# The first MLP product as seven half-size products per pair of columns, and the MLP in two passes through memory

## The chip, the cores and the metric

One NeuronCore of a Trainium2 chip runs the whole layer. The metric is the device time of one execution in microseconds. TensorE (PE) does the matrix products, with its weight loads shown as a lane of their own (PEld); VectorE (DVE) and ScalarE (ACT) do the elementwise work; GpSimd (POOL) has little to do; SyncE (SP) issues the transfers. All arithmetic is in float32: each operand of a product is split into a high part, rounded to the multiplier's format, and the remainder (low part), and every product is made of three matmuls, high times high, high times low and low times high.

## The reference, cut to what matters

The change is in the MLP at the end of the layer; what stands before it (attention, gating, the merge and `w_out`) keeps its arithmetic.

```
# x: (512, 2048) tokens by channels, g_ff: (2048), w_ff1: (2048, 8192), w_ff2: (8192, 2048)
h2 = x * rsqrt(mean(x * x) + EPS) * g_ff          # RMSNorm, one scale per token
x  = x + square(relu(h2 @ w_ff1)) @ w_ff2
```

## The kernel before

The program is written as a flow of tiles; a planner puts the instructions on the engines' queues by a simulated time, in the order of the program where several are ready, and gives out the buffers. Activations lie in slots of 128 partitions by 512 elements (`slot`, 72 in one pool and 10 in another). A weight tile of 512 KB (128 partitions by 1024 elements, `w_raw`) is loaded by SP, ACT rounds it to `w_hi`, DVE subtracts to get `w_lo`; there are six such pieces, so three weight tiles are ready or in use at a time. `mm3` issues the three matmuls of a product (lines 68, 69, 70).

Ahead of the MLP, `w_out` makes the new residual in 16 tiles `x2[tb, j]` (128 tokens by 512 channels, line 562), whose squares are summed (line 564). Each tile is turned (line 577) and split with the gain `g_ff` into `h2T` (lines 106 and 107), channels on the partitions and the 512 tokens along the row. The token scale `rstd_b` (the reciprocal root, lines 584, 585, 213, then 291 to 294) isn't in `h2T`: it is multiplied in later, when a hidden tile leaves PSUM.

The MLP is one loop over 16 chunks of 512 hidden columns. `hidden(f, p)` makes a pair of hidden tiles (2 times 128 columns by 512 tokens) by `by_column`: 16 channel tiles times 2 column tiles times 3 matmuls, each 512 tokens wide, 96 matmuls a pair. A hidden tile is clamped, scaled (line 603) and squared (line 604). `factors` (lines 615 to 618, and the splits 103, 104) makes seven factors of 256 tokens from a pair: the four quarters' three own ones and four sums, as in Winograd's form of Strassen's product. `strassen` multiplies these with seven factors of a block of `w_ff2` (512 hidden rows by 1024 channels): four loads of 512 KB, four sums on DVE (line 165), seven splits (lines 103, 104), and for each factor 12 matmuls 512 channels wide; each factor's result is added from PSUM into the residual tiles (line 643), 16 additions of 128 by 512 a call. So the product with `w_ff1` is direct, the product with `w_ff2` already takes seven parts in eight, and the two alternate: while the factors of one chunk are multiplied, the hidden tiles of the next are made.

The order of the work around the change is this: PE takes its matmuls in the order of the program; DVE and ACT prepare up to three weight tiles ahead; SP's queue is in order, and each load waits for a free `w_raw`.

Of the kernel before, what the change touches and what calls it, by code (L numbers as in the profile page):

```python
# [28 lines left out]
SLOTS = 72  # L29
SPARE = 10  # L30
# [3 lines left out]
def tile_hybrid_layer(ctx: ExitStack, tc: tile.TileContext, x, g_mix, w_in, g_q, g_k, ln_g, ln_b,  # L34
# [10 lines left out]
    before = ExitStack()  # L45
    spare = before.enter_context(tc.tile_pool(name="spare", bufs=SPARE))
# [25 lines left out]
    state = {"load": None}  # L72
# [10 lines left out]
    def weight(wap, kt, c0, w=W):  # L83

        ck = CK * W // w
        raw = wpool.tile([P, ck, w], F32, name="w_raw", tag="w_raw", bufs=3)
# [53 lines left out]
    def strassen(wap, r0, c0, lhs, evac):  # L140

        KH = 2

        def piece(name):
            return wpool.tile([P, KH, W], F32R, name=name, tag="w_piece", bufs=6)

        def whole(name):
            return state["whole"].tile([P, KH, W], F32, name=name, tag="whole")

        def quarter(h, c):
            raw = whole("w_raw")
            state["load"] = nc.sync.dma_start(
                out=raw, in_=wap[r0:r0 + 2 * KH * P, c0 + c * W:c0 + (c + 1) * W]
                .rearrange("(k h p) c -> h p k c", p=P, h=2)[h])
            return raw

        w11, w12, w21, w22 = quarter(0, 0), quarter(1, 0), quarter(0, 1), quarter(1, 1)
        sc = whole("w_sum")

        def plus(o, a, b):
            nc.vector.tensor_tensor(out=o, in0=a, in1=b, op=ALU.add)


        made = {"m7": lambda: plus(w11, w11, w21), "m6": lambda: plus(sc, w11, w22),
                "y22": lambda: plus(w12, sc, w12), "m5": lambda: plus(w21, w21, w22)}
        take = {"y11": w11, "y21": w12, "m7": w11, "m6": sc, "y22": w12, "m4": w22, "m5": w21}  # L170
        banks = {}
        for name, b, first, last in (("y11", 0, True, False), ("y21", 1, True, True),
                                     ("m7", 2, True, False), ("m6", 0, False, False),
                                     ("y22", 1, True, True), ("m4", 2, False, True),
                                     ("m5", 0, False, True)):
            if name in made:
                made[name]()
            hi, lo = piece("w_hi"), piece("w_lo")
            split_to(hi, lo, take[name])
            if first:  # L180
                banks[b] = [(aux if b == 1 else acc)("q") for _ in range(2)]
            for t in range(2):
                o = banks[b][t]
                for k in range(KH):
                    y = [part[:, t * P:(t + 1) * P] for part in lhs(k, name)]
                    mm3(o, y, (hi[:, k, :], lo[:, k, :]), first and k == 0, k == KH - 1,
                        skip_group_check=True)
                evac(name, t, o)
# [82 lines left out]
    def hT_of(k):  # L271

        if k == len(hT):
            t = aux("xT")
            for tb in range(NTB):
                nc.tensor.transpose(out=t[:, tb * P:(tb + 1) * P], in_=xq[tb, k], identity=ident)
            hT.append(split(t, "hT", gT[:, k:k + 1], spare if k < SPARE // 2 else slots))
        return hT[k]
# [264 lines left out]
    for j in range(D // W):  # L543
# [3 lines left out]
        def evac_b(c, o):  # L547
# [3 lines left out]
            mT.append(split(m, "mT", pool=spare if len(mT) >= KT - 4 else slots))  # L551
# [5 lines left out]
    h2T = []  # L557
    ss2 = const.tile([P, NTB, 4], F32, name="ss2")
    for j in range(D // W):
        def evac_x(tb, o):  # L560
            t = x2[tb, j]
            nc.vector.tensor_tensor(out=t, in0=o, in1=t, op=ALU.add)
            sq = slot("sq")
            nc.scalar.activation(out=sq, in_=t, func=AF.Square, accum_out=ss2[:, tb, j:j + 1])

# [8 lines left out]
        def turned(c, j=j):  # L574
# [5 lines left out]
            h2T.append(split(t, "h2T", gT2[:, k:k + 1]))  # L580
# [6 lines left out]
    behind.append(lambda: along(rstd2, rstd_b))  # L587

    before.close()
    state["whole"] = ctx.enter_context(tc.tile_pool(name="whole", bufs=5))  # L590


    HS = S // 2
    PAIRS = 2
    chunks = DFF // (PAIRS * 2 * P)

    def hidden(f, p):

        act = []

        def evac_f(c, o):
            t = slot("relu")
            nc.vector.scalar_tensor_tensor(out=t, in0=o, scalar=0.0, in1=rstd_b, op0=ALU.max, op1=ALU.mult)
            nc.scalar.activation(out=t, in_=t, func=AF.Square)
            act.append(t)

        by_column(w_ff1[0], (f * PAIRS + p) * 2 * P, lambda k: h2T[k], KT, evac_f, "f1", w=2 * P)
        return act

    def factors(act):  # L610
# [3 lines left out]
        m7, m6, m4, m5 = ta[:, :HS], ta[:, HS:], tb[:, :HS], tb[:, HS:]  # L614
        nc.vector.tensor_tensor(out=m7, in0=y12, in1=y22, op=ALU.subtract)
        nc.vector.tensor_tensor(out=m6, in0=m7, in1=y11, op=ALU.subtract)
        nc.vector.tensor_tensor(out=m4, in0=y21, in1=m6, op=ALU.add)
        nc.vector.tensor_tensor(out=m5, in0=y11, in1=y12, op=ALU.subtract)
        y = {}
        for name, src in (("y11", y11), ("y21", y21), ("m7", m7), ("m6", m6), ("y22", y22),  # L620
# [54 lines left out]
```

## Time and profile before

| | |
|---|---|
| median of 3 runs | 2540.3 us (2539.97 to 2541.31) |
| the profiled execution | 2540.31 us |
| its span, first to last instruction | 2538.6 us |
| PE busy | 2520.2 us (99%), 11306 matmuls |
| weight loads (PEld) busy | 2086.5 us (82%) |
| DVE busy | 1550.1 us (61%) |
| ACT busy | 851.6 us (34%) |
| POOL busy | 118.6 us (5%) |
| data moved | 259.83 MB, mean 102 GB/s |

The profile is one execution, taken by the hardware profiler. Its own time is 2540.31 us beside a span of 2538.6 us, so 1.7 us lie outside the span. An engine's busy time is the time in which at least one of its instructions ran. The duration of a matmul is modelled and longer than the time from one matmul's start to the next, since they are pipelined; the distance of starts is what counts for time. The same holds in a smaller measure for DVE and ACT, whose instructions overlap a little.

### The profile page before, as it was taken

The numbers are of one execution on the slowest core, as the hardware profiler recorded it, in microseconds if no ns is written. First come the engines' busy times: TensorE is split into PE (matmuls) and PEld (weight loads), VectorE is DVE, ScalarE is ACT, GpSimd is POOL, SyncE is SP. The second block draws the span as 40 slices with busy tenths as digits, with TensorE's granted clock in tenths as the row PEclk, the third lists the DMA queues.
The fourth block names the chain that finished last, engine by engine and source line by source line (L and its number), as shares of the span: only waits on it lengthen the run. The fifth ranks groups of instructions, "written<-read, shape, count | busy, mean of one in ns | idle before, by whom it ended". The sixth has DMA issues, their size and how long they took to land.

```text
span 2538.6 us, 28443 instructions
## 1 busy us (share of the span) xinstructions
PE 2520.2 (99%) x11306; PEld 2086.5 (82%) x11306; DVE 1550.1 (61%) x2062; ACT 851.6 (34%) x1172; POOL 118.6 (5%) x123
## 2 busy tenths in 40 slices
PE   8999999999999999999999999999999999999998
PEld 7888888888888888888888888888888888888886
DVE  4555463332335343333477877787877877787879
ACT  5333332222223222232333334243333334243332
POOL 0212110000121010100000000000000000000000
PEclk9999999999999999999999999999999999999999
DMA  5322323333333333333433333332333333332323
GB/s 175 92 86 73 91 67 100 92 100 100 109 99 100 94 98 99 116 125 108 125 91 117 99 101 100 100 117 85 114 99 117 99 101 100 100 116 86 114 74 117
DMA packets 169574, 259.83 MB, mean 102 GB/s; under 512 B 8368, under 2 KB 77024, under 8 KB 169440
## 3 DMA queue, kind: packets, MB, share of 16 engines
q1 hardware_dynamic: 169440, 258.01, 33.3%
q8 instruction: 89, 1.46, 0.2%
q14 instruction: 45, 0.37, 0.0%
HBM read 253.78 MB, written 4.19 MB: 102 GB/s over the span
## 4 chain that ended last, share of the span: by engine, by line
PE 96%; DVE 2%; issue 1%; DMA 0%; ACT 0%; POOL 0%; SPq 0%; DVEq 0%; POOLq 0%
PE f L70 9%; PE f L68 9%; PE f L69 9%; PE q L69 9%; PE q L68 9%; PE q L70 9%; PE xo L70 2%; PE xo L69 2%; PE xo L68 2%; PE gb L68 2%; PE gb L70 2%; PE gb L69 2%; PE ga L68 2%; PE ga L69 2%; PE ga L70 2%; PE v L70 1%
## 5 line engine op out<-in xcount | busy, mean ns | idle before, releaser
L92 DVE TENSOR_TENSOR w_lo<-w_raw,w_hi 128x1024 fp32r<-128x1024 f32 x336 | 413.6, 1234 | 672.6 <-ACT w_hi L90 663.8
L90 ACT CAST w_hi<-w_raw 128x1024 fp32r<-128x1024 f32 x336 | 353.9, 1053 | 944.4 <-PE q L69 149.1
L68 PE MATMUL f<-h2T_hi,w_hi 128*128 128x512 f32 x1024 | 398.5, 389 | 0.0
L69 PE MATMUL f<-h2T_lo,w_hi 128*128 128x512 f32 x1024 | 398.3, 389 | 0.0
L70 PE MATMUL f<-h2T_hi,w_lo 128*128 128x512 f32 x1024 | 393.9, 389 | 0.0
L69 PE MATMUL q<-w_lo,ys 128*128 128x512 f32 x896 | 349.9, 391 | 1.6 <-DVE w_lo L104 1.5
L70 PE MATMUL q<-w_hi,ys 128*128 128x512 f32 x896 | 349.3, 390 | 0.0
L103 ACT CAST w_hi<-w_raw 128x1024 fp32r<-128x1024 f32 x192 | 202.0, 1053 | 421.7 <-PE f L69 273.5
L643 DVE TENSOR_TENSOR x<-x,q 128x512 f32<-128x512 f32 x512 | 336.8, 683 | 3.5 <-PE q L70 0.6
L68 PE MATMUL q<-w_hi,ys 128*128 128x512 f32 x896 | 325.5, 390 | 4.2 <-ACT w_hi L103 4.2
L104 DVE TENSOR_TENSOR w_lo<-w_raw,w_hi 128x1024 fp32r<-128x1024 f32 x192 | 234.9, 1224 | 133.5 <-ACT w_hi L103 133.5
L70 PEld LDWEIGHTS f<-h2T_hi,w_lo 128*128 128x128 f32 x1024 | 192.3, 188 | 39.9
L69 PEld LDWEIGHTS f<-h2T_lo,w_hi 128*128 128x128 f32 x1024 | 192.3, 188 | 39.8
L68 PEld LDWEIGHTS f<-h2T_hi,w_hi 128*128 128x128 f32 x1024 | 192.2, 188 | 39.7
L68 PEld LDWEIGHTS q<-w_hi,ys 128*128 128x128 f32 x896 | 168.6, 188 | 40.2 <-ACT w_hi L103 5.4
L69 PEld LDWEIGHTS q<-w_lo,ys 128*128 128x128 f32 x896 | 168.7, 188 | 38.8 <-DVE w_lo L104 3.9
L70 PEld LDWEIGHTS q<-w_hi,ys 128*128 128x128 f32 x896 | 168.7, 188 | 34.8
L68 PE MATMUL gb<-hT_hi,w_hi 128*128 128x512 f32 x256 | 100.3, 392 | 0.2 <-DVE gb L413 0.2
L68 PE MATMUL xo<-w_hi,mT_hi 128*128 128x512 f32 x256 | 100.5, 393 | 0.0
L68 PE MATMUL ga<-hT_hi,w_hi 128*128 128x512 f32 x256 | 100.4, 392 | 0.0
L69 PE MATMUL ga<-hT_lo,w_hi 128*128 128x512 f32 x256 | 100.0, 391 | 0.0
L70 PE MATMUL ga<-hT_hi,w_lo 128*128 128x512 f32 x256 | 99.9, 392 | 0.0
(199 smaller groups left out, 3690.0 us busy)
## 6 DMA issues: line engine op xcount, KB each, us to landing
w_raw<-in_w_ff_dram SPq DMA_DIRECT2D x256, 512.0 KB, 3.7
w_raw<-in_w_in_dram SPq DMA_DIRECT2D x144, 512.0 KB, 3.7
w_raw<-in_w_out_dram SPq DMA_DIRECT2D x32, 512.0 KB, 3.7
w_raw<-in_w_oa_dram SPq DMA_DIRECT2D x16, 512.0 KB, 3.7
w_raw<-in_w_ob_dram SPq DMA_DIRECT2D x16, 512.0 KB, 3.7
x<-in_x_dram SPq DMA_DIRECT2D x16, 256.0 KB, 5.4
out_dram<-x SPq DMA_DIRECT2D x16, 256.0 KB, 2.0
xq<-in_x_dram SPq DMA_DIRECT2D x12, 256.0 KB, 6.5
```

The lines of the kernel that those rows point to most:

```text
L68: nc.tensor.matmul(o, lhsT=lh[0], rhs=rh[0], start=start, stop=False, **kw)
L69: nc.tensor.matmul(o, lhsT=lh[0], rhs=rh[1], start=False, stop=False, **kw)
L70: nc.tensor.matmul(o, lhsT=lh[1], rhs=rh[0], start=False, stop=stop, **kw)
L90: nc.scalar.copy(out=hi, in_=raw)
L92: nc.vector.tensor_tensor(out=lo, in0=raw, in1=f32(hi), op=ALU.subtract)
L103: nc.scalar.copy(out=hi, in_=src)
L104: nc.vector.tensor_tensor(out=lo, in0=src, in1=f32(hi), op=ALU.subtract)
L643: nc.vector.tensor_tensor(out=a, in0=a, in1=o, op=op)
```

## The change

Both MLP products are made of seven half-size products, and the MLP is two passes: first all of `w_ff1`, then all of `w_ff2`.

**First pass.** The normalized activations need the token scale before they are used, so `x2T` (turned, with the gain) is multiplied by `rstd_b` and cut into seven factors `hs` for each pair of channel tiles (128 rows by 256 tokens each). The first pair of hidden tiles is made directly, by matmuls 256 tokens wide, from the factors that need no sums; then the four sums are made for all eight pairs of channel tiles. Each of the other 31 pairs goes through `strassen_columns`: the weights of a block of 2048 rows by 256 columns come as four tiles of 512 KB (rows of 128 elements), the factors of the weights are made by three additions on DVE and one addition done by a transfer (`accum_op`, issued by POOL, onto the tile `w21`), seven splits, and 7 times 24 matmuls 256 tokens wide. Their results leave PSUM by four ACT copies and four DVE additions of 128 by 256; the hidden pair is clamped, squared, cut into its seven factors, and these are written to memory (`keep_hidden`, 7 writes of 256 KB a pair). The residual tiles are written to memory too (`kept`).

**Second pass.** `strassen_tokens` takes chunks of 1024 hidden rows by 1024 channels: two weight blocks whose results add up in PSUM, so each result is added into the residual once for 1024 hidden rows. The hidden factors of the next chunk are read back between the products (`fetch`), and the residual tiles are read back at the start of the pass.

The core of the diff:

```diff
-SLOTS = 72
-SPARE = 10
+SLOTS = 64
+LONG = 12
+SHORT = 6
...
+    BANK = {"y11": (0, True), "y21": (1, True), "m7": (2, True), "m6": (0, False), "y22": (3, True),
+            "m4": (2, False), "m5": (0, False)}
...
+        def parts(self, name):
+            if name == "m7":
+                nc.vector.tensor_tensor(out=self.a, in0=self.w11, in1=self.w21, op=ALU.add)
+
+                nc.gpsimd.dma_start(out=self.w21, in_=self.blocks[1, 1], accum_op=ALU.add)
+            if name == "m6":
+                nc.vector.tensor_tensor(out=self.c, in0=self.a, in1=self.w22, op=ALU.add)
+            if name == "y22":
+                nc.vector.tensor_tensor(out=self.w12, in0=self.c, in1=self.w12, op=ALU.add)
+            src = self.take[name]
+            hi, lo = piece("w_hi"), piece("w_lo")
...
+    def strassen_columns(wap, c0, rhs, evac):
+
+        KH = KT // 2
+        blocks = {(h, c): wap[:, c0 + c * P:c0 + (c + 1) * P].rearrange("(k h p) c -> h p k c", p=P, h=2)[h]
+                  for h in range(2) for c in range(2)}
+        w = Sums(blocks, [state["raw"].tile([P, KH, P], F32, name="w_raw", tag="w_raw") for _ in range(6)])
...
+            o = banks[b][:, :HS]
+            for k in range(KH):
+                mm3(o, (hi[:, k, :], lo[:, k, :]), rhs[name][k], new and k == 0, k == KH - 1,
+                    skip_group_check=True)
+            evac(name, o)
...
+            for i in range(2):
+                hi, lo = ws[i].parts(name)
+                for t in range(2):
+                    for k in range(KQ):
+                        y = [part[:, t * P:(t + 1) * P] for part in lhs[name][i * KQ + k]]
+                        mm3(banks[b][t], y, (hi[:, k, :], lo[:, k, :]), new and i == 0 and k == 0,
+                            i == 1 and k == KQ - 1, skip_group_check=True)
...
-            h2T.append(split(t, "h2T", gT2[:, k:k + 1]))
+            keep = slot("x2T")
+            nc.scalar.activation(out=keep, in_=t, func=AF.Copy, scale=gT2[:, k:k + 1])
+            x2T.append(keep)
...
-    behind.append(lambda: along(rstd2, rstd_b))
+    flush()
+    along(rstd2, rstd_b)
...
+    for b in range(KT):
+        y = x2T[b]
+        nc.vector.tensor_tensor(out=y, in0=y, in1=rstd_b, op=ALU.mult)
+        for half in range(2):
+            name = "y" + "12"[b % 2] + "12"[half]
+            far = name == "y11" or name == "y21" and b // 2 < LONG - KT // 2
+            hs[name, b // 2] = halves(y[:, half * HS:(half + 1) * HS], long if far else slots)
...
+        for i, name in enumerate(NAMES):
+            nc.sync.dma_start(out=store[p // GROUP][i, p % GROUP], in_=f32(ys[name, 0]))
...
+    for k in range(KT // 2):
+        factors(hs, x2T[2 * k:2 * k + 2], k)
+    keep_hidden(0, act)
...
+    for p in range(1, DFF // (2 * P)):
+        hidden(p)
...
+    first.close()
+    second = [ctx.enter_context(tc.tile_pool(name=n, bufs=6)) for n in ("raw2", "more2")]
+    state["raw"], state["more"] = second
+    lhs = {name: fetch(0, name) for name in NAMES}
+    for tb in range(NTB):
+        for j in range(D // W):
+            t = slot("x2")
+            nc.sync.dma_start(out=t, in_=kept[tb, j])
+            x2[tb, j] = t
```

## Rows read from the trace of the kernel before

**Rows 1.** The page's head and its busy time by engine.
```profile
span 2538.6 us, 28443 instructions
...
PE 2520.2 (99%) x11306; PEld 2086.5 (82%) x11306; DVE 1550.1 (61%) x2062; ACT 851.6 (34%) x1172; POOL 118.6 (5%) x123
```

**Rows 2.** Stretches of the span: engines' busy time, clock, DMA share, GB/s.
```profile
6.00:12.00 6.00, 3.51 (x13) 2.82 (x14) 3.28 (x4) 2.45 (x4) 0.00 (x0) 1.00 1.04 344
...
1297.00:1338.00 41.00, 41.00 (x182) 33.96 (x182) 30.80 (x44) 15.01 (x21) 0.00 (x0) 1.00 0.29 89
...
2466.00:2500.00 34.00, 28.78 (x118) 22.33 (x117) 33.37 (x55) 14.19 (x24) 0.00 (x0) 0.93 0.24 71
```

**Rows 3.** Groups by line in the MLP: matmuls of either product (one line of three).
```profile
L68 PE MATMUL f<-h2T_hi,w_hi 128*128 128x512 f32 x1024 | 398.5, 389 | 0.0
...
L68 PE MATMUL q<-w_hi,ys 128*128 128x512 f32 x896 | 325.5, 390 | 4.2 <-ACT w_hi L103 4.2
```

**Rows 4.** Timeline of PE where the MLP begins: start, duration, instruction.
```profile
1215.18 0.39 PE L68 MATMUL f<-h2T_hi,w_hi 128*128 128x512 f32 x1
...
1215.86 0.39 PE L68 MATMUL f<-h2T_hi,w_hi 128*128 128x512 f32 x1
```

**Rows 5.** Timeline of PE in attention, around three matmuls 256 wide.
```profile
160.60 0.29 PE L68 MATMUL z<-kT_hi,qT_hi 128*128 128x256 f32 x1
...
160.97 0.22 PE L68 MATMUL z<-kT_hi,qT_hi 128*128 128x128 f32 x1
```

**Rows 6.** Timeline of the weight loads in the position mixing.
```profile
782.61 0.19 PEld L527 LDWEIGHTS mix<-wsp,vn_hi 128*128 128x128 f32 x1
...
783.07 0.19 PEld L527 LDWEIGHTS mix<-wsp,vn_hi 128*128 128x128 f32 x1
```

**Rows 7.** Timeline and tile rows of the token scale, last residual tile to `rstd_b`.
```profile
1215.38 0.69 DVE L562 TENSOR_TENSOR x<-xo,x 128x512 f32<-128x512 f32 x1 [0.67 <-PE xo L70]
...
1218.03 1.02 POOL L213 TENSOR_TENSOR rstd<-ms,mhalf 128x4 f32<-128x4 f32 x1 [178.62 <-DVE ms L585]
...
L291 DVE TENSOR_SCALAR dg<-ident,rstd x4: 276/278/280, 1230.5 to 1231.1; 128x128 f32<-128x128 f32 x4
...
1236.25 0.69 DVE L294 COPY rstd_b<-rp 128x512 f32<-128x512 f32 x1 [0.61 <-PE rp L293]
```

**Rows 8.** Timeline of DVE late in the MLP.
```profile
2462.05 1.23 DVE L104 TENSOR_TENSOR w_lo<-w_raw,w_hi 128x1024 fp32r<-128x1024 f32 x1 [0.56 <-ACT w_hi L103]
...
2473.65 0.42 DVE L615 TENSOR_TENSOR m<-relu 128x256 f32<-128x256 f32 x1
2473.99 0.42 DVE L618 TENSOR_TENSOR m<-relu 128x256 f32<-128x256 f32 x1
...
2480.06 1.28 DVE L643 TENSOR_TENSOR x<-x,q 128x512 f32<-128x512 f32 x2
2481.26 1.22 DVE L104 TENSOR_TENSOR w_lo<-w_raw,w_hi 128x1024 fp32r<-128x1024 f32 x1
2482.39 0.42 DVE L617 TENSOR_TENSOR m<-relu,m 128x256 f32<-128x256 f32 x1
```

**Rows 9.** Timeline of ACT in the MLP: casts, then clamp and square.
```profile
2470.09 0.71 ACT L103 CAST ys<-relu 128x256 fp32r<-128x256 f32 x2
2470.70 0.71 ACT L103 CAST ys<-m 128x256 fp32r<-128x256 f32 x2
...
1322.78 0.63 ACT L604 ACTIVATE relu<-relu 128x512 f32<-128x512 f32 x1 [3.15 <-DVE relu L603]
1324.06 1.05 ACT L103 CAST w_hi<-w_raw 128x1024 fp32r<-128x1024 f32 x1 [0.66 <-PE f L69]
```

**Rows 10.** The page's DMA issues: tile, count, size, us from issue to landing.
```profile
w_raw<-in_w_ff_dram SPq DMA_DIRECT2D x256, 512.0 KB, 3.7
...
out_dram<-x SPq DMA_DIRECT2D x16, 256.0 KB, 2.0
```

**Rows 11.** Timeline of PE at the end: the last matmul.
```profile
2533.35 0.39 PE L70 MATMUL q<-w_hi,ys 128*128 128x512 f32 x1
```

More of the change, by code (lines that the diff above doesn't have):

```diff
@@ L138, in by_column @@
             evac(c, o[c])
[L140 to L170, printed above, removed]
-        banks = {}
[L172 to L181, printed above, removed]
-            for t in range(2):
[L183 to L188, printed above, removed]
@@ new lines, in tile_hybrid_layer, with keep_hidden @@
+    GROUP = 4
+    chunks = DFF // (GROUP * 2 * P)
+    store = [dram.tile([len(NAMES), GROUP, P, W], F32, name=f"store{f}") for f in range(chunks)]
+    def keep_hidden(p, act):
+        for a in act:
+            nc.scalar.activation(out=a, in_=a, func=AF.Square)
+        ys = {}
+        for name, src in (("y11", act[0][:, :HS]), ("y21", act[1][:, :HS]), ("y22", act[1][:, HS:])):
+            ys[name, 0] = halves(src)
+        factors(ys, act, 0)
+        for i, name in enumerate(NAMES):
+            nc.sync.dma_start(out=store[p // GROUP][i, p % GROUP], in_=f32(ys[name, 0]))
@@ new lines, in tile_hybrid_layer @@
+    o = [acc("f1") for _ in range(2)]
+    for kt in range(0, KT, 4):
+        hi, lo = weight(w_ff1[0], kt, 0, 2 * P)
+        for c in range(2):
+            for k in range(4):
+                a = [part[:, k, c * P:(c + 1) * P] for part in (hi, lo)]
+                for half in range(2):
+                    name = "y" + "12"[k % 2] + "12"[half]
+                    mm3(o[c][:, half * HS:(half + 1) * HS], a, sides(hs[name, (kt + k) // 2]),
+                        kt + k + half == 0, kt + k == KT - 1, skip_group_check=True)
@@ new lines, in tile_hybrid_layer, with fetch @@
+    for p in range(1, DFF // (2 * P)):
+        hidden(p)
+    def fetch(f, name):
+        ts = []
+        for p in range(GROUP):
+            t = slot("ys", F32R)
+            nc.sync.dma_start(out=f32(t), in_=store[f][NAMES.index(name), p])
+            ts.append(sides(t))
+        return ts
+    first.close()
+    second = [ctx.enter_context(tc.tile_pool(name=n, bufs=6)) for n in ("raw2", "more2")]
+    state["raw"], state["more"] = second
+    lhs = {name: fetch(0, name) for name in NAMES}
@@ L630, in tile_hybrid_layer @@
              "m5": [(1, 1, ALU.subtract), (1, 0, ALU.add)]}
-    ahead = [hidden(0, p) for p in range(PAIRS)]
+    done = {"y21": [(0, 0)], "m4": [(0, 1)], "m5": [(1, 1), (1, 0)]}
     for f in range(chunks):
-        ys = [factors(act) for act in ahead]
-        ahead = []
+        ahead = {}
         for g in range(2):
-            if f < chunks - 1:
-                ahead.append(hidden(f + 1, g))
             def evac_y(name, t, o):
```

130 lines of the change are left out of this document (94 added, 36 removed).

## The prediction, made before the changed kernel was run

> **What bounds the kernel now.** I read the page's head first: PE is busy 99% of the span, so only matmul time, or a wait that stops PE, can move the end [rows 1]. Busy time hides how dense the matmuls are, so next I read PE's timeline. Three matmuls 512 wide take 0.68 us from start to start, 0.2267 us each, at a granted clock of 1.00 [rows 2, 4]. The MLP has 3 times 1024 matmuls for `w_ff1` and 3 times 896 for `w_ff2` [rows 3], 5760 in all, 1305.6 us at that distance. It begins at 1215.2 [rows 4] and the span ends at 2538.6 [rows 1]: 1323.4 us, so 17.8 us are not matmuls of this kind. Of those, 4.9 us follow the last matmul's start [rows 11]. Most of the rest lies near the end: in a stretch of 34 us DVE is busy 33.4 and PE only 28.8 [rows 2], because no `w_ff1` product is left beside which DVE could work ahead. In a stretch within the loop DVE has 30.8 of 41 us [rows 2]. So: PE bounds the MLP, DVE is second, and transfers are far behind (89 GB/s at a share of 0.29, where an early stretch moves 344 GB/s at a full share) [rows 2].
>
> **The pair of hidden columns, where the gain must come from.** A direct pair is 96 matmuls of 512: 21.8 us. A changed pair is 7 times 24 = 168 matmuls of 256, seven eighths of the columns but 1.75 times the instructions, each with its weight load. What counts is the distance of matmuls 256 wide. Half of 0.2267 is 0.113. In attention, three of them take 0.37 us to the start of the next, 0.123 each, with changes of width at both ends [rows 5]. In the position mixing, where the matmuls are too short to hide their loads, four loads take 0.46 us, 0.115 each [rows 6]. I take 0.119, between the two, and keep 0.113 and 0.123 as bounds: 20.0 us a pair (19.0 to 20.7), 1.8 us less than now, 55 us over 31 pairs.
>
> The loads' recorded 0.19 us each [rows 6] overlap, or their starts could not stand 0.115 apart; that the load would bind at 0.19 is a rival below. The Trainium skill (TensorE: Matmul & The Clock Gate, LDWEIGHTS) puts a load at columns over 1.2 GHz, 107 ns for 128, and its section on the back-to-back gap puts 256 columns at 262 cycles, 109 ns. By that a pair would be 18.3 us and my sum 51 us lower; rows 4 to 6 have every distance longer than its formula, so the measurement decides.
>
> **What else a pair asks.** Distances of DVE starts: 0.34 us for 128 by 256, 0.60 for 128 by 512, 1.13 for 1024 elements [rows 8]. A pair has three sums and seven remainders of 1024 and 15 operations of 256 (four additions from PSUM, four factors, seven remainders): 10 x 1.13 + 15 x 0.34 = 16.4 us, 82% of 20.0. ACT: seven casts at 1.05, 11 of 256 at 0.31, four of 512 at 0.63 [rows 9] make 13.3 us. Transfers: four loads, the accumulating one, seven writes, 4.25 MB (1024-based, 4.46 million bytes) in 20 us are 223 GB/s, two thirds of 344. All are below PE's time, so I cost them at nothing and let PE cover them; DVE's 3.6 us of slack is the thinnest cover. On SP's queue the seven writes wait for DVE's remainders and stand before later loads, but six weight buffers give nearly a pair of lead. The accumulating transfer on POOL's queue, otherwise empty, has no row in this trace. It must land between the sum for `m7` and the cast for `m5`, four products or 11.4 us. From below, a load of that size lands in 3.7 us [rows 10]; from above nothing bounds it. I take under 11 us, since the load row is the nearest, and keep the other end as a rival.
>
> **The second pass** has 16 half chunks of 168 matmuls of 512, 2688 as now: 609.3 us. DVE per half chunk: 20 x 1.13 + 16 x 0.60 = 32.2 of 38.1 us, where two calls of today would need 44 (22 x 1.13 + 32 x 0.60); so the loss at the end of the kernel goes. Transfers, 8.5 MB (8.9 million bytes) in 38.1 us, are 234 GB/s. This costs nothing by itself.
>
> **The start of the MLP, which gets worse.** Today the scale is multiplied in late, and PE goes from `w_out` straight into `w_ff1`. After the change every factor needs `rstd_b`. From the rows: last residual tile at 1215.4, POOL's power from 1218.0 to 1219.05, four products of 0.28 spread over 0.9 us, eight short matmuls of about 1 us in all, a copy of 0.69 [rows 7]: about 1222. Then multiply, cast and remainder of the first tile, 1.5 us. PE stands still 8.5 us. From 1222 DVE has 16 x (0.60 + 2 x 0.34) = 20.5 us for the plain factors, 8 x 8 x 0.34 = 21.8 for the sums and their splits, 11 x 0.34 = 3.7 for the first pair's own factors, and 16.4 for the next pair: 62.4 us, while PE has 192 x 0.119 + 20.0 = 42.8. DVE bounds these two pairs; they end 63 us after 1222, at 1285. In the late stretch, where PE waits for DVE, the mean granted clock is 0.93, so part of it ran at 1.2 instead of 2.4 GHz [rows 2]; for the two gaps here I add 3 us: 1288 (1280 to 1298).
>
> **Between the passes** the first products need factors, weights and residual tiles, some 15 MB (16 million bytes), 46 us at 344 GB/s. Buffers come free from the last pair's second product on (14 us ahead), and the products that use them last 38 us. I put 6 us of wait, between 0 and 30 for nothing hidden.
>
> **The sum**, on the span of the profiled execution: 1288 + 30 x 20.0 + 6 + 609.3 + 4.9 = 2508, plus the 1.7 us outside the span: 2510. The profiled execution (2540.31) is at the median (2540.3), so nothing is scaled. The gain of 55 us and some 11 us saved at the end are eaten up by about 30 us at the start and 6 between the passes.
>
> **Rivals.**
> *The accumulating transfer comes late (slower).* Place: POOL's queue in the first pass. ACT takes its casts in order, so a late `m5` also holds the next pair's. The price is one microsecond a pair, 31 us in all, for each microsecond beyond the window of 11.4 us (17 with the two products that are prepared ahead); it decides once a pair takes 1.0 us more than I forecast (30 us over 31 pairs). At 3 us beyond, 2600. For it: four times the pieces of today's `w_ff2` load (128 elements each), and no row of any transfer on POOL's queue. Against it: the load's 3.7 us [rows 10]. Chance 0.13. The Trainium skill (SBUF — State Buffer, Who interferes with whom) says that VectorE in a two-port mode locks GpSimd out of writing descriptors, but that a two-input `tensor_tensor`, which is nearly all that DVE does here, contends only with GpSimd's reads; no run here shows it yet.
>
> *DVE becomes the bound of a pair.* Its 16.4 us count no waits. Behind a sum, the remainder waits 0.56 us for ACT's cast [rows 8]; three of those, and a tail of clamp, square and cast (about 1.6 us on ACT) that nothing fills, make 20 us, and with PE's waits 21.5: 1.5 x 30 = 45 us more, 2555. For it: DVE at 98% with PE at 85% in the late stretch [rows 2]. Against it: the planner fills such waits in the loop now. Chance 0.11.
>
> *The change of passes or the start isn't hidden.* If the weights stand behind all factors and residual tiles in SP's order, 11.5 MB (12 million bytes) take 35 us before the first product: 2540, no change. Chance 0.09.
>
> *Weight loads bind.* At 0.19 us a matmul [rows 6] a pair is 31.6 us: 31 x 11.6 more, 2870. Rows 5 speak against it. Chance 0.02.
>
> *Better than forecast.* At 0.113 and no wait between the passes: 2474. Chance 0.04.
>
> **How the numbers follow.** The forecast has 0.61, and its own range is 2482 to 2532 (0.113 to 0.123 a matmul is -30 to +20 us, the start -8 to +10, the change of passes -6 to +24, not all at once). To leave out no more than 2 in 10, the range reaches to 2575, which takes in the DVE case and the start case; beyond it lies the late transfer. A measurement tells 0.2%, about 5 us, from no change. Faster 0.65 (forecast and better case), same 0.08 (most of the start case), slower 0.27 (late transfer, most of the DVE case, loads, and the rest).
>
> **What would show it.** In the new profile: matmuls 256 wide at 0.117 to 0.121 us, pairs 20 us apart with PE idle near nothing; POOL's transfer landing in under 11 us with no ACT wait on it at `m5`; a gap of 8 to 9 us on PE near 1216 and a second one of some 15 us before the first `m7`; DVE near full from 1222 to 1285; a DMA share near 0.65 in both passes; the last half chunks as dense as the others. Pairs of 21 us or more, or PE waits on DVE or on the transfer all through the first pass, would prove me wrong.

## The result, and the profile after

The changed kernel takes 2552.2 us (median of 5 runs, 2549.47 to 2552.93) against 2540.3 before: 1.0044 times as long, 95% interval 1.0029 to 1.0058. I forecast 2510 and faster; it is slower, by more than the 0.2% that a measurement tells from no change. The profiled execution took 2549.47 us, so 39.5 us lie between forecast and trace.

The page's head and busy times of the changed kernel, beside [rows 1]:

```profile
span 2547.8 us, 35037 instructions
...
PE 2485.3 (98%) x13634; PEld 2165.9 (85%) x13634; DVE 1608.8 (63%) x2116; ACT 1041.3 (41%) x1517; POOL 205.1 (8%) x186
```

PE's busy time fell by 34.9 us, yet the span grew by 9.2: PE now stands still, or runs at a lower clock, somewhere. Stretches of the span of the changed kernel show where (columns as in [rows 2]):

```profile
1264.00:1292.00 28.00, 13.43 (x64) 10.01 (x63) 27.62 (x72) 16.16 (x42) 1.60 (x1) 0.71 0.41 98
...
1320.00:1880.00 560.00, 560.00 (x4669) 560.00 (x4668) 472.32 (x698) 360.00 (x614) 41.89 (x27) 1.00 0.83 222
...
1906.00:1922.00 16.00, 1.09 (x10) 0.89 (x8) 10.38 (x18) 6.62 (x13) 1.20 (x1) 0.65 0.99 317
1922.00:1960.00 38.00, 35.08 (x134) 27.64 (x135) 19.48 (x22) 10.52 (x10) 0.00 (x0) 0.88 1.03 375
1960.00:2000.00 40.00, 37.59 (x163) 29.93 (x162) 32.91 (x37) 14.65 (x14) 2.42 (x2) 1.00 1.05 358
2000.00:2500.00 500.00, 500.00 (x2208) 414.01 (x2207) 441.51 (x476) 194.25 (x184) 33.40 (x28) 1.00 0.75 227
```

Both passes are dense once they run: 560 of 560 us and 500 of 500. The losses are at their edges: 14.6 us of 28 within the first changed pair (its first matmul starts at 1259.47), with DVE full; 14.9 of 16 between the passes, with the DMA engines full from there to 2000; and a granted clock of 0.71, 0.65 and 0.88 in the three stretches at 1264, 1906 and 1922.

The pair itself, in PE's timeline (first and last of 21 matmul starts) and by ACT's copies, which come once a pair:

```profile
1400.05 0.28 PE L72 MATMUL q<-ys,w_hi 128*128 128x256 f32 x1
...
1402.45 0.28 PE L72 MATMUL q<-ys,w_hi 128*128 128x256 f32 x1
...
1332.58 0.65 ACT L712 ACTIVATE relu<-q 128x256 f32<-128x256 f32 x2
...
1352.74 0.65 ACT L712 ACTIVATE relu<-q 128x256 f32<-128x256 f32 x2
```

20 distances in 2.40 us are 0.1200 us a matmul, and a pair takes 20.16 us, against the 0.119 and 20.0 of the forecast. The matmuls are as I thought; 30 pairs cost 4.8 us more.

The accumulating transfer, on the page's list of DMA issues (us to landing last, as in [rows 10]):

```profile
store<-ys SPq DMA_DIRECT2D x224, 256.0 KB, 4.9
ys<-store SPq DMA_DIRECT2D x224, 256.0 KB, 5.4
w_raw<-in_w_ff_dram POOLq DMA_DIRECT2D x63, 512.0 KB, 7.0
```

It lands in 7.0 us at the median, under the 11 that I had taken.

The start, in the timelines of POOL, PE and DVE (beside [rows 7]):

```profile
1220.15 1.73 POOL L175 DMA_DIRECT2D w_raw<-in_w_ff_dram  x1 [180.15 <-ACT x2T L624]
1221.27 1.69 POOL L254 TENSOR_TENSOR rstd<-ms,mhalf 128x4 f32<-128x4 f32 x1
...
1223.43 2.04 PE L334 MATMUL rp<-dg,ones 128*128 128x128 f32 x8 [4.53 <-DVE dg L332]
1235.14 0.58 PE L73 MATMUL f<-ys,w_hi 128*128 128x256 f32 x1 [6.93 <-DVE ys L108]
...
1256.80 0.60 ACT L697 ACTIVATE relu<-f 128x512 f32<-128x512 f32 x1 [1.91 <-PE f L74]
...
1254.92 1.23 DVE L108 TENSOR_TENSOR w_lo<-w_raw,w_hi 128x1024 fp32r<-128x1024 f32 x1 [4.53 <-ACT w_hi L107]
1256.18 1.23 DVE L179 TENSOR_TENSOR w_raw<-w_raw 128x1024 f32<-128x1024 f32 x1
1257.32 0.42 DVE L643 TENSOR_TENSOR m<-x2T 128x256 f32<-128x256 f32 x1
...
1291.00 0.58 PE L72 MATMUL q<-ys,w_hi 128*128 128x256 f32 x1 [3.58 <-ACT relu L712]
```

The reader is to see three delays. POOL's power (line 254) comes at 1221.27, behind the issue of the first accumulating transfer, and `rstd_b` is ready about 1226.2, not 1222; the power itself takes 1.69 us against 1.02 in [rows 7], and the eight matmuls of line 334, behind a wait of 4.53 us, take 2.04 us against about 1. DVE, which I had full from there on, waits 4.53 us in one place, with the first sum of factors (line 643) only at 1257.32, when the first pair's first clamp on ACT (line 697) is done. And PE's waits in between end at 1291.

Between the passes, SP's queue (weight loads at line 167, stores of factors at 681, fetches at 730) and the first matmul of the second pass:

```profile
1903.36 10.05 SPq L167 DMA_DIRECT2D w_raw<-in_w_ff_dram  x6
1916.28 1.72 SPq L681 DMA_DIRECT2D store<-ys  x3
1918.09 0.98 SPq L730 DMA_DIRECT2D ys<-store  x1
1919.21 2.37 SPq L681 DMA_DIRECT2D store<-ys  x4
1921.68 18.92 SPq L730 DMA_DIRECT2D ys<-store  x27
...
1922.55 0.79 PE L72 MATMUL q<-w_hi,ys 128*128 128x512 f32 x1 [15.46 <-DMA ys<-store]
```

The first fetch goes out at 1918.09, 11 us after the last product of the first pass, behind weight loads and the last pair's stores.

To split the loss for every kernel below I use one rule, on the profiled execution: the first pass ends 0.12 us after its last matmul's start; what the span has beyond that end and beyond 614.2 us (609.3 + 4.9 of the forecast) is called the loss between the passes, though it holds whatever the second pass and the end of the kernel lose as well. Here the last start is 1906.81, so the first pass ends at 1906.9, the second pair (30 pairs of 20.16 earlier) at 1302.1, and the loss is 2547.8 - 1906.9 - 614.2 = 26.7. Against the forecast: start 1302.1 - 1288 = 14.1, pairs 4.8, between the passes 26.7 - 6 = 20.7; together 39.6 of the 39.5 us.

Not all of the 26.7 us is standing still. From 1906 to 2000 PE is idle 20.2 of 94 us. Behind the gap matmuls of 512 stand 0.427 us apart, which is 512 columns at 1.2 GHz, until the one at 1931.04; at 0.2 us each, 18 of them cost some 3.6 us more:

```profile
1924.00 0.63 PE L72 MATMUL q<-w_hi,ys 128*128 128x512 f32 x1
1924.42 0.63 PE L73 MATMUL q<-w_lo,ys 128*128 128x512 f32 x1
```

### The profile page after: what moved, and what is told of

The parts are those of the page before. It is cut to its first block, busy times and chain, and to the rows that moved or that the text cites. A ratio compares the mean times of both kernels' runs of the same rounds, so it can differ in the third digit from the quotient of the medians.

```text
span 2547.8 us, 35037 instructions
## 1 busy us (share of the span) xinstructions
PE 2485.3 (98%) x13634; PEld 2165.9 (85%) x13634; DVE 1608.8 (63%) x2116; ACT 1041.3 (41%) x1517; POOL 205.1 (8%) x186
## 5 line engine op out<-in xcount | busy, mean ns | idle before, releaser
L107 ACT CAST w_hi<-w_raw 128x1024 fp32r<-128x1024 f32 x441 | 464.5, 1054 | 616.4 <-PE q L73 561.0
L96 DVE TENSOR_TENSOR w_lo<-w_raw,w_hi 128x1024 fp32r<-128x1024 f32 x212 | 263.1, 1241 | 606.2 <-ACT w_hi L94 583.9
L108 DVE TENSOR_TENSOR w_lo<-w_raw,w_hi 128x1024 fp32r<-128x1024 f32 x441 | 538.7, 1222 | 166.1 <-ACT w_hi L107 165.8
L94 ACT CAST w_hi<-w_raw 128x1024 fp32r<-128x1024 f32 x212 | 223.0, 1052 | 683.7 <-PE ga L73 99.6
L72 PE MATMUL q<-ys,w_hi 128*128 128x256 f32 x1736 | 493.0, 285 | 7.3 <-ACT relu L712 3.6
L73 PE MATMUL q<-ys,w_hi 128*128 128x256 f32 x1736 | 492.7, 285 | 6.8 <-DVE ys L108 6.8
L74 PE MATMUL q<-ys,w_lo 128*128 128x256 f32 x1736 | 488.4, 284 | 0.6 <-DVE w_lo L108 0.6
L74 PE MATMUL q<-w_hi,ys 128*128 128x512 f32 x896 | 350.0, 391 | 0.0
L72 PEld LDWEIGHTS q<-ys,w_hi 128*128 128x128 f32 x1736 | 329.1, 190 | 9.0 <-ACT ys L107 4.3
L73 PEld LDWEIGHTS q<-ys,w_hi 128*128 128x128 f32 x1736 | 329.1, 190 | 8.2 <-DVE ys L108 8.1
L72 PE MATMUL q<-w_hi,ys 128*128 128x512 f32 x896 | 315.3, 391 | 17.3 <-DMA ys<-store 16.2
L74 PEld LDWEIGHTS q<-ys,w_lo 128*128 128x128 f32 x1736 | 327.1, 190 | 0.8 <-DVE w_lo L108 0.8
L175 POOL DMA_DIRECT2D w_raw<-in_w_ff_dram x63 | 86.5, 1373 | 1368.8 <-DVE w_raw L173 659.2
L755 DVE TENSOR_TENSOR x<-x,q 128x512 f32<-128x512 f32 x256 | 167.8, 681 | 10.8 <-PE q L74 7.0
```

Source lines behind the costliest of these rows:

```text
L72: nc.tensor.matmul(o, lhsT=lh[0], rhs=rh[0], start=start, stop=False, **kw)
L73: nc.tensor.matmul(o, lhsT=lh[0], rhs=rh[1], start=False, stop=False, **kw)
L74: nc.tensor.matmul(o, lhsT=lh[1], rhs=rh[0], start=False, stop=stop, **kw)
L94: nc.scalar.copy(out=hi, in_=raw)
L96: nc.vector.tensor_tensor(out=lo, in0=raw, in1=f32(hi), op=ALU.subtract)
L107: nc.scalar.copy(out=hi, in_=src)
```

## Experiments

All start from the changed kernel; where an edit stands on an earlier one, the text says so. Times are medians; each profiled execution, from which the two columns on the right come, lies within 3 us of its median.

| kernel | us | first pass ends | loss between the passes |
|---|---|---|---|
| forecast | 2510 | 1888 | 6 |
| changed kernel | 2552.2 | 1906.9 | 26.7 |
| sum of weights by DVE, no accumulating transfer | 2552.7 | 1908.4 | 28.6 |
| two direct pairs | 2554.1 | 1910.8 | 26.6 |
| sums ahead of the clamps | 2546.4 | 1902.8 | 26.1 |
| sums by name, clamps last | 2543.8 | 1900.3 | 28.7 |
| sums by name, clamps between | 2534.6 | 1891.0 | 25.0 |
| all 28 fetches early | 2553.7 | 1907.0 | 30.1 |
| 12 fetches early | 2550.4 | 1907.3 | 26.8 |
| volume spread | 2545.8 | 1907.2 | 24.2 |
| order by need | 2550.2 | 1907.0 | 27.5 |
| spread and order | 2535.6 | 1906.5 | 12.9 |
| both stages | 2519.6 | 1891.9 | 11.9 |

### What paces a matmul 256 wide

```diff
-                mm3(o, (hi[:, k, :], lo[:, k, :]), rhs[name][k], new and k == 0, k == KH - 1,
-                    skip_group_check=True)
+                n = HS if k == 0 else 224
+                mm3(o[:, :n], (hi[:, k, :], lo[:, k, :]), [y[:, :n] for y in rhs[name][k]], new and k == 0,
+                    k == KH - 1, skip_group_check=True)
```

> In the first pass, the seven products use only 224 of the 256 tokens for every k but the first; the products of the other 32 tokens are left out, number of matmuls and of weight loads stays the same. In the changed kernel the pair of hidden columns takes 20.16 us, 168 matmuls at 0.1200 us, with the weight loads on record as busy all the time. Theory A, the weight load paces the 256 wide matmuls: the pair stays at 20.1 to 20.2 us and the time at 2548 to 2555 us. Theory B, the columns pace them: 0.1200 us falls to about 0.107 (224 of 256, with some fixed part), a pair takes 17.9 to 18.4 us and the time falls by 52 to 66 us, to 2486 to 2500 us.

2517.5 us, one run. Neither theory: a pair takes 19.06 us. So I narrowed it further, with 192 in the same line. Both kernels leave out products, and are there only for the distance of matmuls.

> As the run with 224 tokens, now with 192 of the 256 tokens for every k but the first; the products of the other 64 tokens are left out. So far in the steady first pass: 0.1200 us a matmul at 256 columns, 0.1115 at 224; and 0.2267 at 512. Theory A, two limits: a matmul costs its columns at 2.4 GHz plus about 13 ns (256: 106.7 + 13.3; 512: 213.3 + 13.3; 224 would be 106.7), and the weight load sets a floor of about 0.111: 192 columns stay at 0.110 to 0.112. Theory B, only one cost that falls with the columns (8.5 ns for 32): 192 columns give 0.102 to 0.104 us.

2521.3 us, one run, and a pair of 19.04. PE's timeline with 224 tokens (21 distances), then with 192 (20):

```profile
1402.31 0.27 PE L72 MATMUL q<-ys,w_hi 128*128 128x224 f32 x1
...
1404.65 0.29 PE L72 MATMUL q<-ys,w_hi 128*128 128x256 f32 x1
```

```profile
1402.16 0.27 PE L73 MATMUL q<-ys,w_hi 128*128 128x192 f32 x1
...
1404.39 0.31 PE L72 MATMUL q<-ys,w_hi 128*128 128x256 f32 x1
```

2.34 / 21 and 2.23 / 20 are 0.111 us in both: from 224 columns down the distance no longer falls. That is a floor from a second limit, which I take to be the one load for each matmul. At 256 columns the matmul itself is the limit, just above the floor. From 256 to 512 columns the distance grows by 0.1067 us, which is 256 columns at 2.4 GHz; 0.1200 is these 106.7 ns and 13.3 ns more, and 0.2267 is 213.3 and the same 13.3. By that 224 columns would stand 0.107 us apart, so the 0.111 is not the columns' doing. Two halves cost one such 13.3 ns more than one whole: 0.2400 instead of 0.2267.

That the floor belongs to the load and not to the matmul has support in the kernel before. In the position mixing matmuls 128 and 256 wide alternate:

```profile
782.60 0.22 PE L529 MATMUL mix<-wsp,vn_lo 128*128 128x128 f32 x1
782.66 0.34 PE L527 MATMUL mix<-wsp,vn_hi 128*128 128x256 f32 x1
```

Here one matmul starts 0.06 us behind another, while the loads stand 0.115 us apart [rows 6]. So matmuls can follow each other faster than 0.111 us, and it is not their own start that sets the floor. The lane of weight loads of the changed kernel is shown as busy 560 of 560 us in the pass where it isn't the limit; it can't be read as one. The Trainium skill (TensorE: Matmul & The Clock Gate, Back-to-back issue gap) gives 262 cycles for 256 columns, 109 ns at full clock, as the gap of a matmul by itself, and says that this counts too little for small widths in a stream with loads, which the prediction left out. In these runs, with a load for each, it is 120, so the measurement decides. By its formula for the load (section LDWEIGHTS), columns over 1.2, I estimate 107 ns for 128 columns, 4 ns under the floor seen here.

### The accumulating transfer

```diff
-                nc.gpsimd.dma_start(out=self.w21, in_=self.blocks[1, 1], accum_op=ALU.add)
...
+            if name == "m5":
+                nc.vector.tensor_tensor(out=self.w21, in0=self.w21, in1=self.w22, op=ALU.add)
```

> The transfer that adds the fourth block of weights onto the third in memory, on POOL's queue, is left out, and DVE adds the two tiles itself ahead of the product m5 (one more DVE addition of 1024 elements, 1.13 us, a pair and a half chunk; 512 KB less to move each time, 33 MB in all). Theory A, the accumulating transfer costs nothing in the first pass: pair still 20.16 us, DVE at 90% and not the bound; the MLP starts up to 4 us earlier, since POOL's power no longer stands behind that transfer, and some DMA time is freed between the passes: 2540 to 2553 us. Theory B, DVE becomes the bound with 17.5 of 20.16 us plus its waits: a pair of 20.6 to 21.3 us, 2565 to 2590 us.

2552.7 us (ratio to before 1.0047, 1.0030 to 1.0063), the copies of line 712 still 20.16 apart, DVE at 497.9 of 560 us. Theory A: neither the transfer nor DVE binds a pair. Without the transfer on its queue, POOL's power started at 1219.22 instead of 1221.27, and the first direct product at 1225.55 instead of 1227.42; yet the first pass ended no earlier (1908.4). What is early there is lost behind it; how was not followed up.

### The start

The first idea was that PE lacks work while DVE makes the sums, so it got a second direct pair:

```diff
+    acts = [clamped(direct(p)) for p in range(2)]
...
-    keep_hidden(0, act)
+    for p, act in enumerate(acts):
+        keep_hidden(p, act)
...
-    for p in range(1, DFF // (2 * P)):
+    for p in range(2, DFF // (2 * P)):
```

> Two pairs of hidden columns, not one, are multiplied directly before the factor sums are made, so that PE has 43 us of work while DVE makes the sums. It costs PE 24 more matmuls of 256 (192 against 168), 2.9 us. Theory A: at the start DVE bounds the first pairs and PE stands still for about 27 us between 1227 and 1291; with a second direct pair most of the idle time from 1264 to 1291 is filled: 10 to 15 us less after the 2.9 us are paid, 2537 to 2543 us. Theory B: the start is bound by DVE's total work (62 us of factors and remainders before the third pair), which stays; PE then waits as long one pair later, and the time is 2550 to 2556.

2554.1 us (1.0055, 1.0040 to 1.0070), the time of theory B, but not for its reason. ACT's clamp of the second direct pair, the first sum on DVE, and two stretches of this kernel:

```profile
1275.47 0.60 ACT L703 ACTIVATE relu<-f 128x512 f32<-128x512 f32 x1 [1.95 <-PE f L74]
...
1275.95 0.42 DVE L643 TENSOR_TENSOR m<-x2T 128x256 f32<-128x256 f32 x1
...
1240.00:1264.00 24.00, 24.00 (x203) 24.00 (x202) 10.18 (x13) 7.88 (x12) 1.73 (x1) 1.00 0.32 78
...
1292.00:1320.00 28.00, 10.45 (x35) 7.84 (x36) 24.28 (x65) 13.18 (x36) 1.56 (x1) 0.51 0.51 150
```

DVE was not full: it was busy 10.18 of 24 us while PE did the extra pair, since the sums start only when the first clamp of that pair is done, as they did behind the first pair's at 1257.32. In both kernels a remainder and a sum of weights stand right ahead of them in DVE's queue, and that remainder waited for ACT's cast (1254.92 in the changed kernel), so the rows don't tell which of the two held the sums. PE's hole moved to 1292. So the next edit writes the sums ahead of the clamps:

```diff
+    o = direct(0)
     for k in range(KT // 2):
         factors(hs, x2T[2 * k:2 * k + 2], k)
-    keep_hidden(0, act)
+    keep_hidden(0, clamped(o))
```

> The first pair's two clamps are written behind the factor sums instead of ahead of them, nothing else moves. In the changed kernel DVE is idle from 1250.3 to 1257.3, and the first factor sum starts at 1257.32, right behind the first pair's clamps on ACT. Theory A: the sums wait for buffers or order behind the clamps, so they now start at about 1250 and the start is shorter by 5 to 7 us: 2545 to 2547 us. Theory B: DVE's sums wait for something else (the planner puts them there), and nothing changes: 2550 to 2554.

2546.4 us (1.0023, 1.0013 to 1.0033), theory A: the first pass ends 4.1 us earlier. (DVE was not idle for the whole stretch that the expectation names: it did a remainder and a sum from 1254.92 on.) DVE's timeline, the first sum and the one for the last `k`:

```profile
1246.86 0.42 DVE L643 TENSOR_TENSOR m<-x2T 128x256 f32<-128x256 f32 x1
...
1276.73 0.42 DVE L643 TENSOR_TENSOR m<-x2T 128x256 f32<-128x256 f32 x1
```

The sums now start at 1246.86, but the product `m7`, PE's third, needs `m7` of all eight `k`, and the last comes at 1276.73: `factors` makes four names for a `k` before it goes on. So the same sums were made name by name.

```diff
-    for k in range(KT // 2):
-        factors(hs, x2T[2 * k:2 * k + 2], k)
+    for name, dst, i, j, op in (("m7", 3, 1, 3, ALU.subtract), ("m6", 3, 3, 0, ALU.subtract),
+                              ("m4", 2, 2, 3, ALU.add), ("m5", 1, 0, 1, ALU.subtract)):
+        for k in range(KT // 2):
+            y = [t[:, half * HS:(half + 1) * HS] for t in x2T[2 * k:2 * k + 2] for half in range(2)]
+            nc.vector.tensor_tensor(out=y[dst], in0=y[i], in1=y[j], op=op)
+            hs[name, k] = halves(y[dst])
```

> Built on the version with the factor sums ahead of the clamps (2546.4 us): the 32 factor sums of the first pass are made name by name, all of m7 first, then m6, m4, m5, instead of four at a time for each k; they overwrite the tiles of the operands that are done with. DVE does the same number of operations. Theory A: what stops PE from 1264 to 1291 is the order, since m7 is complete only when the last k is done; with m7 complete after a quarter of the work PE goes on through m7, m6, y22, m4, m5, the second pair ends 10 to 15 us earlier, and the clock does not fall a second time: 2531 to 2538 us. Theory B: DVE's total work bounds the two pairs as I predicted, in any order, and the time stays at 2544 to 2548.

2543.8 us (1.0009, 1.0000 to 1.0018), outside theory A and 0.2 us under theory B: the first pass ends 2.5 us earlier, not 10 to 15. PE's timeline has two waits left:

```profile
1274.48 0.58 PE L72 MATMUL q<-ys,w_hi 128*128 128x256 f32 x1 [5.50 <-ACT relu L703]
...
1283.93 0.58 PE L72 MATMUL q<-ys,w_hi 128*128 128x256 f32 x1 [4.86 <-ACT relu L725]
```

Both wait for copies out of PSUM on ACT, whose queue is in order: the first copy stood behind the casts of the sums, the second behind those of the first pair's own factors. In the last form the clamps follow `m7`, the other sums are written inside the second pair, and the first pair's own factors behind it.

```diff
+    make("m7")
+    act0 = clamped(o)
...
+            if p == 1 and name in ("y11", "y21", "m7"):
+                make({"y11": "m6", "y21": "m4", "m7": "m5"}[name])
...
+        if p == 1:
+            keep_hidden(0, act0)
         keep_hidden(p, act)
```

> Factor sums name by name again, now with m7 ahead of the first pair's clamps, and m6, m4, m5 written inside the second pair behind its products y11, y21 and m7; the first pair's own factors behind the second pair's products. Nothing else moves. With the sums name by name and the clamps behind all of them (2543.8 us) PE waited 5.5 and 4.9 us on two PSUM copies of ACT that stood behind 17 to 26 casts. Theory A: these copies were the remaining wait; PE is idle under 4 us in all from 1240 to the end of the second pair, which ends at 1283 to 1288 instead of 1301.5: 2533 to 2540 us. Theory B: the start is bound by DVE's total, and whatever is won is lost again when pair three waits for the first two pairs' factors and buffers: 2542 to 2547.

2534.6 us (0.9978, 0.9969 to 0.9987), theory A. The first pass ends at 1891.0, so the second pair at 1286.2, and the same operations are done. Of the 15.9 us since the changed kernel, 0.9 lie ahead of the MLP: `rstd_b` is ready at 1225.3 here, though nothing before it was edited. Stretches of this kernel:

```profile
1240.00:1264.00 24.00, 24.00 (x202) 24.00 (x201) 24.00 (x58) 12.99 (x27) 0.00 (x0) 1.00 0.08 23
1264.00:1292.00 28.00, 24.13 (x180) 23.12 (x179) 28.00 (x57) 19.70 (x45) 1.60 (x1) 0.94 0.57 148
```

Now DVE is full, 52 of 52 us, and PE has 24.13 of 28 at a clock of 0.94, where it had 13.43 at 0.71. From `rstd_b` to the end of the second pair DVE is busy 60.9 of 60.9 us here, and 63.6 of 75.9 in the changed kernel. That DVE bounds these two pairs is what I had forecast, for 1288; it fits this order only. PE is nearly full as well (48.1 of 52 us from 1240 on), so another order of DVE's work could take out only some 4 us of waits there.

### Between the passes

The fetches of the second pass's first chunk were put ahead of the last pair's stores, all 28 or the first 12:

```diff
+        if p == DFF // (2 * P) - 1:
+            lhs.update({name: fetch(0, name) for name in NAMES})
         keep_hidden(p, act)
```

> All 28 fetches of the second pass's first chunk are issued in the last hidden pair, ahead of that pair's own seven stores in program order, instead of behind them. In the changed kernel the last matmul of the first pass stands at 1906.2 us, the first of the second pass at 1922.55, and about 27 us of PE's time are lost between 1906 and 1965 (the second pass takes some 621 us instead of 609.3, plus the gap of 15.5). Theory A, order on SP's queue: the fetches wait behind stores that wait for the last pair's remainders; with the fetches ahead the first matmul of the second pass comes some 12 us earlier, about 2552 - 12 to 2552 - 20 = 2532 to 2540 us. Theory B, volume: 16 MB must land before the products can run, at 375 GB/s whatever the order; the gain is under 5 us, 2547 to 2553. A third outcome: the weights of the first half chunk now stand behind 28 fetches, and the gap stays with weights as its cause (2550 to 2560).

> Only the 12 fetches of the first three products' factors are put ahead of the last pair's stores; the other 16 stay where they are, so that the weights of the second pass stand behind 12 transfers and not 28. Theory A (order): as much gain as with all 28, or 2 to 4 us more since weights come earlier: 2530 to 2540 us. Theory B (volume): no gain, 2547 to 2553. If this gains and the version with all 28 does not, the weights' place behind the fetches is what counts.

2553.7 us (1.0054, 1.0039 to 1.0069), the third outcome, and 2550.4 (1.0041, 1.0026 to 1.0056), theory B: the order of the fetches alone is not it. With all 28, SP's queue and PE:

```profile
1904.17 17.76 SPq L709 DMA_DIRECT2D ys<-store  x23
1922.32 0.99 SPq L167 DMA_DIRECT2D w_raw<-in_w_ff_dram  x2
...
1929.53 2.17 PE L72 MATMUL q<-w_hi,ys 128*128 128x512 f32 x4 [20.02 <-ACT w_hi L107]
```

The factors are there and the weights come late: the same engines, full at 365 GB/s, only serve something else first. So volume was taken out: half of the residual tiles and the second chunk's factors move to where they are needed.

```diff
+                if f == 0 and g == 0 and i < NTB:
+                    for j in range(2, 4):
+                        back(i, j)
+                if f == 0:
+                    if g == 1:
+                        ahead[name] = fetch(1, name)
+                    return
```

> Between the passes the same transfers are made, but later: the residual tiles of the columns that the second half chunk needs (8 of 16, 2.1 MB) are read during the first half chunk, and the factors of the second chunk (20 of 28 fetches, 5.2 MB, that now go out in the first half chunk) during the second half chunk. Order in the queue alone did not help (two versions with earlier fetches: 2553.7 and 2550.4 us). Theory B, volume: in the changed kernel 33.6 MB move in the 94 us from 1906 to 2000 at a full share, and PE loses about 20 us of these; with 7.3 MB taken out of the first half chunk 10 to 19 us come back, 2533 to 2543 us. Theory C, the first matmul of the second pass is late by its own chain (stores, fetch, weights) and the rest is small: the 15.5 us gap stays and the gain is under 6 us, 2546 to 2553 us.

2545.8 us (1.0022, 1.0013 to 1.0032): 6.4 less by the medians, 2.5 less loss by the profiles, between the theories and nearer C. The gap to the first matmul stays at 15.8 us. Then both, this edit and the transfers of the first half chunk in the order in which its products need them:

```diff
+    for i, (name, tiles) in enumerate((("y11", ((0, 0), (1, 0))), ("y21", ()), ("m7", ((2, 1), (3, 1))),
+                                       ("m6", ((0, 1), (1, 1))), ("y22", ((2, 0), (3, 0))), ("m4", ()), ("m5", ()))):
+        for w in ws0 if i < 4 else ():
+            w.load(i)
+        lhs[name] = fetch(0, name)
+        for tb, j in tiles:
+            back(tb, j)
+        if name == "y21":
+            keep_hidden(DFF // (2 * P) - 1, last)
```

> As the version that spreads the transfers later (2545.8 us), and besides the transfers of the first half chunk are issued in the order in which its products need them: the two first blocks of weights, the four tiles of y11, two residual tiles, then the blocks for y21, and so on; the last pair's seven stores come behind y21. In the changed kernel the DMA engines are full from 1898 on, 8 us before PE runs dry, and the 15.5 us gap to the first matmul of the second pass has eight weight loads (4.2 MB) and 14 stores (3.7 MB) ahead of the first four fetches, where the first product needs 2.1 MB. Theory: with volume and order both put right the gap falls to 3 to 8 us, no wait over 2 us comes after it, and the time is 8 to 14 us below that version: 2532 to 2538. Rival: the early blocks must wait for buffers of the first pass (SP waits 11.6 us for a matmul of the last pair at one load), order in the program changes nothing, 2543 to 2550.

2535.6 us (0.9981, 0.9972 to 0.9990), within the theory's 2532 to 2538: the loss is 12.9, with one wait of 7.2 us and one of 0.8. The last run takes the spread away again and keeps the order.

> The order of the first half chunk's transfers by need alone (blocks of weights two by two, the fetches of each product behind them, the last pair's stores behind y21), with the residual tiles of the second half chunk and the second chunk's factors at their old places. So far: neither 2552.2 us, volume spread alone 2545.8, both 2535.6. Theory A, the two add: order alone is worth the 10 us that it brought on top of the spread, 2540 to 2544 us. Theory B, it works only where the volume is out of the way: 2547 to 2553, as with the two versions that only fetched earlier. Theory C, order is all and the spread brings nothing on top: 2535 to 2538.

2550.2 us (1.0038, 1.0025 to 1.0051): theory B. PE and SP's queue of this run:

```profile
1916.70 2.17 PE L72 MATMUL q<-w_hi,ys 128*128 128x512 f32 x4 [7.26 <-ACT w_hi L107]
...
1972.10 2.17 PE L72 MATMUL q<-w_hi,ys 128*128 128x512 f32 x4 [13.99 <-ACT w_hi L107]
...
1947.70 12.70 SPq L743 DMA_DIRECT2D ys<-store  x20
1960.80 4.44 SPq L174 DMA_DIRECT2D w_raw<-in_w_ff_dram  x7
```

The first gap is halved as with both, and what was won is lost 55 us later: the second half chunk's weights stand behind 20 fetches for the second chunk, on engines that are still full (386 GB/s from 1940 to 1975). Order decides who waits first, volume how much is waited in all. By the medians order alone gives 2.0 us, which lies within the spread of the changed kernel's runs, and volume alone 6.4, both together 16.6; by the loss in the profiles the two alone give nothing and 2.5.

### Both stages

The last form of the start and the spread and ordered change of passes in one kernel.

> Both edits together, the start by names and the change of passes by deadline. If the two stages are independent, the gains add: 2552.2 less 14 to 18 at the start and 15 to 20 between the passes is 2514 to 2523 us, 0.7 to 1.0% below the kernel before (2540.3). If a gain at the start only moves the wait to the change of passes (with the factors ready earlier, the first matmul of the second pass stayed at 1918), the sum is smaller: 2525 to 2538.

2519.6 us (0.9916, 0.9902 to 0.9930), as expected (2514 to 2523), and faster than the kernel before and the changed one. The parts were worth 17.6 and 16.6 us alone and are worth 32.6 together, so the stages are nearly independent. The page of this kernel, and PE's largest wait between the passes:

```profile
span 2518.0 us, 35021 instructions
...
PE 2478.6 (98%) x13634; PEld 2163.6 (86%) x13634; DVE 1606.7 (64%) x2116; ACT 1039.0 (41%) x1517; POOL 205.1 (8%) x186
...
1901.85 2.17 PE L72 MATMUL q<-w_hi,ys 128*128 128x512 f32 x4 [7.46 <-ACT w_hi L107]
```

The same number of matmuls, and the 2510 of the forecast is 9.6 us away: 4.8 in the pairs, 5.9 between the passes, and a start about 1 us better.

## Why the prediction was wrong

**What bounds the kernel, the pair, the second pass.** Right. The gain is in the pair, with matmuls 0.1200 us apart (0.119 forecast) and nothing that stops PE in 560 us. DVE's 16.4 of 20.0 us (82%) measured 84%, ACT's 13.3 measured 64%, the transfers' 223 GB/s measured 222. The second pass is dense to near its end, where the kernel before lost. The term for the pair was mis-sized by 0.16 us, 4.8 in all. One reading was off without weight: the last matmul before starts 5.25 us ahead of the span's end, and the 4.9 us count from its recorded end.

**The start: the step that failed is "DVE bounds these two pairs; they end 63 us after 1222, at 1285".** With 3 us for the clock the forecast was 1288, at most 1298; the second pair ended at 1302.1. I added up DVE's operations and let them follow one another without a gap, as if their order were the one in which PE asks. Three things replaced it. `rstd_b` came 4 us late, partly since POOL's power stood behind the accumulating transfer (some 2 us of it, by the run without that transfer); the prediction calls POOL's queue "otherwise empty", and the power is on it. The sums stood behind the first pair's clamps in the program, which cost some 4 us. And `m7` was complete only with the last `k`, while ACT's PSUM copies stood behind the casts; with both put right the second pair ended at 1286.2. The 62.4 us of work were right (DVE is busy 63.6 us from `rstd_b` to the second pair's end); what failed is that they follow one another without a gap, since DVE stood idle 12.3 us there. Only the order of the last run fills DVE. That its 1286.2 lies so near 1288 is in part luck: `rstd_b` still came 3 us later than forecast, and the second pair's own factors, which I had counted in, can only follow that pair's products (DVE makes them from 1291.5 on).

**Between the passes: the step that failed is "I put 6 us of wait, between 0 and 30".** The loss was 26.7 us, 15.5 of it one wait. I set 46 us of transfers against 14 + 38 us of cover, as one sum. The trace has 33.6 MB in the 94 us from 1906 (the GB/s of the three stretches), since the second chunk's factors are fetched in the same stretch and the last pair's stores come first; and the first product waits for what is queued ahead of its 2.1 MB, not for the sum. The range had held this: 26.7 is near its upper end.

**Rivals.** The accumulating transfer came in 7.0 us, and no engine waits for it from 1320 to 1880: refuted. DVE as the bound of a pair: refuted at 84%, and still at 89% with one addition more. Weight loads at 0.19: refuted; a floor lies at 0.111, which I put down to them. The one that happened is the change of passes or the start not being hidden, to which I gave 0.09 and 2540 us: both parts of it came at once, and its time was 12 us short. Its mechanism, weights behind all factors and residual tiles, is not what came: the weights were first in the queue, and the first product waited for its factors behind them.

**Still open.** The 7.5 us wait for the first weights of the second pass remains in the best version, and so does PE's 6.93 us wait near 1235, where DVE does 14 multiplications before the first remainder; neither was tried. That the floor at 0.111 is the weight load is argued, from the one load per matmul and from the mixing; no run varies the load alone.

## What to carry to other kernels

A total of work for an engine that sets a stage's end is its time only if the order of production is the order of use: where a consumer needs one name for all `k`, make that name for all `k` first, and look at what stands ahead of PSUM copies on an in-order queue. Where a kernel changes from one stage to the next, list the transfers by the moment each is needed, prefetches for the stage after included; here full DMA engines were relieved by order and volume together, and much less by one of them. Halving a matmul's width adds its fixed part once more: here 168 halves stand for 84 whole matmuls, and 84 times 13.3 ns are 1.1 us of the 2.7 that seven products for eight would have saved in a pair of 21.8.

## What the runs showed of the hardware that I had not expected

Matmuls of 512 and 256 columns share a fixed part of 13.3 ns at full clock (0.2267 and 0.1200 us), and 224 and 192 columns both take 0.111 us with one weight load each. At the lower clock there is no such part to see: 0.427 us for 512 columns is the columns at 1.2 GHz alone. The loads' lane was busy 560 of 560 us without being the limit. The granted clock fell with PE's waits and added to them: 0.71 in the stretch of the first changed pair, 0.50 in the 4 us from 1914 between the passes, with 0.88 on average in the 38 us after the first product came.
